# Three edits in the order of a hybrid decoder step: two heads' masked statistics change engine, one weight computation and one merge change step

## The chip, the cores and the metric

The kernel runs on one core of a Trainium2 chip. The metric is the device time of one execution in microseconds (us). The engines named below are TensorE (PE; its weight loads are shown as PEld), VectorE (DVE), ScalarE (ACT), GpSimd (POOL) and SyncE (SP), whose queue issues the DMA transfers of this kernel. Each engine works through its own list of instructions in the order in which the program wrote them.

## The reference

One layer of a decoder for a prompt of 2048 positions (width 1024) and for a sample group of 8 x 4 rows. The parts that the change is near:

```python
q, k, v, u, vg = _project(x, norm1_g, w_in)          # RMSNorm and one projection
for (w, d), bias_hj in zip(BRANCHES, biases):        # windows (128,1), (512,4), (2048,16)
    o, l = _dilated_prompt(q, k, v, bias_hj, d, w // d + 1)   # softmax(q k / 8 + bias) v, and its log-sum-exp
    outs.append(o); lses.append(l)
w = jax.nn.softmax(jnp.stack(lses, axis=0), axis=0)  # merge weights of each position and head
att = jnp.sum(w[..., None] * jnp.stack(outs, axis=0), axis=0)
x = x + jnp.concatenate([att, u * gate], axis=-1) @ w_out
x = x + _swiglu(x, norm2_g, w_gate, w_up, w_down)
```

There are 8 heads of 64 columns. After the layer comes a last RMSNorm. New key, value and gate caches are outputs too.

## The kernel before

**Stages.** Projection and gating come first (to some 430 us of the trace), then the attention of the sample group and of the prompt (to about 880 us), the output projection with the second RMSNorm (to about 960 us), and the feed-forward part, which goes through three blocks of positions (6, 6 and 4 tiles of 128) and takes the rest.

**How the attention is tiled.** The kernel folds the first two branches into one band of at most 5 tiles of 128 keys, and keeps the third, strided one apart; so each head has 16 band items (one for every 128 queries) and 4 strided items (4 residues of 16 each). A list holds all items of the 8 heads, 20 to a head, and item number i starts at step `B0 + i`. Heads are numbered 0 to 7; head 7 is the last one. Its list interleaves them: band 0, strided 0, band 1, strided 1, and so on to strided 3, then bands 4 to 15. Below, x is the step of head 7's first item, and L = x + 19 that of its last.

**What sets the order.** Every piece of work is registered with a step and a phase; the phases within a step are, in this order, early, exp, low, scores, turn, mid, values, out, misc, store. The plan sorts by step, phase and order of registration, and writes the instructions out in that order for all engines. So a piece registered earlier stands ahead on every engine that it uses, and an instruction that has to wait holds up what stands behind it on its engine.

**A band item.** Its scores (L856, PE into the two-buffer tile `ps_s`) come at its own step, the bias with the row minimum (L862, DVE) one step later, the exponential with the row sum (L867, ACT) two later, the transposition (L883, PE into a ring of three banks) three later with a copy of its first three blocks by ACT (L888), and of the others by DVE four later (L894). After each fourth band the products with the values follow (L911, PE, in two parts), and ACT copies them to the tile `ob` (L920). **A strided item** has POOL gather its keys and queries three steps ahead (L927, three casts into `sq`), scores (L935, PE), bias and minimum (L940, L942, DVE), a subtraction (L947, POOL), the exponential (L950, ACT), sums (L954, DVE), a transposition (L959, PE; L961, ACT), products (L971, PE) and a copy (L981, ACT).

**Statistics of a head** (class `Stats`). They bring the band's minima and sums into the strided item's layout and make the merge weights. Their pieces are: `a`, one product of the statistics with a selection mask into `sm` (L997, 128x256 for all 16 tiles of positions, 128x128 for 8 of them), on the engine named by its argument `eng`; `b`, four small matmuls (L1003, PE); `c`, four small DVE instructions (L1010 to L1013); `weights_e`, an exponential (L1016, ACT); `weights_b`, five small DVE instructions (L1021 to L1025); `store`, four DMA stores of the weights to the DRAM tensor `f_d` (L1031, SP). Heads 0 to 6 do this once. Head 7 does it in two halves: positions 0 to 1023 (`r0` is 0) at steps x+14 to x+16, positions 1024 to 2047 (`r0` is 64) at L+3 to L+6.

**The merge.** `merge_load` brings the weights back, spread over the partitions, a quarter of the positions (`ch`) at a time (L1045, SP). `merge` multiplies the band's and the strided output with them and adds (L1054, L1056, L1058), and `merge_store` writes the attention rows to the DRAM tensor `cat_d` (L1063, SP). Its last 128 rows are those of heads 6 and 7. For head 7, quarter 0 is merged by DVE and quarter 1 by POOL.

**The way into the output projection.** Tile 0 of `cat_d` is read by `load_cat` (L1340) without those last rows at step L-3, tiles 1 to 4 by `early_cat` (L1350): 7 of their 8 row groups long ahead, and the last one when head 7's first two quarters have been stored. `split_early` (L1357 ACT, L1358 DVE) and `split_cat` (L1364, L1365) make a high and a low part, in two halves of four row groups. PE multiplies them with `w_out` (L1373 to L1375): tile 0 in pieces from step L+2 on, then from step L+7 on `first_block` with tile 1, 2, 3, the rest of tile 0, 4 and 5. The parts of `w_out` are loaded (L1313) and split (L135 ACT, L138 POOL) from step L-12 on.

Of the kernel before, what the change touches and what calls it, by code (L numbers as in the profile page):

```python
# [23 lines left out]
KD = D // P  # L24
H = 8
# [17 lines left out]
class Plan:  # L43
# [8 lines left out]
    def at(self, step, phase, fn, *args):  # L52
        self.events.append((step, self.PHASES.index(phase), self.n, fn, args))
        self.n += 1
# [10 lines left out]
def hymba_step(ctx: ExitStack, tc: tile.TileContext, A: dict, O: dict):  # L65
    nc = tc.nc
    sync, act, dve, pool, pe = nc.sync, nc.scalar, nc.vector, nc.gpsimd, nc.tensor
# [7 lines left out]
    turn = [0, 0, 0, 0]  # L75
# [85 lines left out]
    at = plan.at  # L161
# [517 lines left out]
    for half in range(2):  # L679
        for ki, kind in enumerate(ORDER[half]):  # L680
            for gi, tiles in enumerate(GROUPS):
# [13 lines left out]
                for j, tj in enumerate(tiles):  # L695
                    t = half * 8 + tj
                    e, ph = e0 + 2 * j, "out"
                    if last:
                        e, ph = e0, "early"
                    elif third:  # L700

                        e, ph = (e0 + 2 * j + 2, "out") if j < 2 else (e0, "early")
# [45 lines left out]
    i = 0  # L748
# [44 lines left out]
    heads, loads, sts, fs, obs, o3s, spare = {}, {}, {}, {}, {}, {}, {}  # L793
# [333 lines left out]
    L = B0 + len(items) - 1  # L1127
# [13 lines left out]
            at(s0 + 5, "misc", finish_load, h)  # L1141
    def stats_of(h, steps, r0, r1):
        d = {}
        at(*steps[0], lambda: d.update(s=Stats(h, sts[h], r0, r1, dve if r0 else pool)))
        for (y, ph), fn in zip(steps, "a b c weights_e weights_b store".split()):
            at(y, ph, lambda fn=fn: getattr(d["s"], fn)())

    for h in range(H):

        s0 = B0 + (h + 1) * NI  # L1150
        end = h == H - 1
        ahead = h == H - 2
        if end:

            x = s0 - NI
            stats_of(h, [(x + y, ph) for y, ph in ((14, "early"), (14, "turn"), (15, "early"), (16, "early"), (16, "early"), (16, "mid"))], 0, 64)
            steps = ((2, "early"), (2, "turn"), (3, "early"), (4, "early"), (5, "early"), (5, "early"))
            at(x + 18, "mid", merge_load, h, 0)
            for part in range(3):
                at(x + 20 + part, "store", merge, h, 0, dve, part)  # L1160
                at(x + 21 + part, "store", merge, h, 1, pool, part)
            at(x + 24, "store", merge_store, h, 0, 2)
        else:
            steps = ((2, "misc"), (3, "misc"), (4, "early"), (5, "early"), (5, "misc"), (6, "mid"))

            for ch, (a, b) in enumerate(((8, 11), (8, 14), (11, 17), (11, 24) if ahead else (11, 20))):
                if ch % 2 == 0:
                    at(s0 + a, "mid", merge_load, h, ch)
                for part in range(3):
                    at(s0 + b + part, "store", merge, h, ch, pool, part)  # L1170
            if ahead:
                at(s0 + 17, "store", merge_store, h, 0, 2)
                at(s0 + 27, "store", merge_store, h, 2, 4)
            else:
                at(s0 + 23, "store", merge_store, h, 0, 4)
        stats_of(h, [(s0 + y, ph) for y, ph in steps], 64 if end else 0, P)
    for i, it in enumerate(items):
        x, h, n = B0 + i, it["h"], it["n"]
# [550 lines left out]
    B = blocks[0]  # L1729
# [40 lines left out]
    at(L + 1, "misc", split_cat, B, 0)  # L1770
    for i, y in ((1, -10), (2, -10), (3, -8), (4, -5)):
        at(L + y, "store", early_cat, B, i, 0, KD - 1)
        at(L + 5, "store", early_cat, B, i, KD - 1, KD)
    for j, ss in enumerate(((0, 1), (2,), (3,), (4, 5), (6,))):
        at(L + 2 + j, "misc", open_part, B, 0, ss, j == 0, False)

# [8 lines left out]
    h = H - 1  # L1785
# [150 lines left out]
    for bi, B in enumerate(blocks):  # L1936
# [8 lines left out]
        part = 4  # L1945
# [172 lines left out]
```

## Time and profile before

| what | value |
|---|---|
| device time, median of 3 runs | 2518.91 us (2518.27 to 2525.55) |
| device time of the profiled execution | 2524.36 us |
| its span, first to last instruction | 2522.5 us |
| PE busy | 2442.2 us, 97% of the span |
| DVE, ACT, POOL busy | 1269.3, 1129.8, 1291.3 us |
| mean granted TensorE clock | 0.988 |
| DMA, mean over the span | 181 GB/s |

A row of the timeline gives the start, the duration, the engine, the line of the kernel, the operation, what it writes and reads, and in square brackets the idle time of its engine just before, with what ended it. Consecutive instructions of one kind are put together (x4). The stretches give, for each engine, its busy time and its count of instructions, then the TensorE clock that was granted (1.00 is full), the DMA share and rate. Span and device time differ by what lies around the first and the last instruction, here 2524.36 - 2522.5 = 1.9 us.

### The profile page before, as it was taken

How to read it: one execution, taken by the hardware profiler on the slowest of the kernel's cores; microseconds unless marked ns; L12 is line 12 of the kernel's file. 1: busy time of each engine (PE TensorE's matmuls, PEld its weight loads, DVE VectorE, ACT ScalarE, POOL GpSimd, SP SyncE). 2: the span in 40 equal slices, each digit the busy share in tenths (PEclk: the TensorE clock that was granted, in tenths of full speed). 3: DMA queues.
4: the chain of work that ended last, by engine and by line, in shares of the span. 5: the costliest groups of instructions: out<-in, count | busy, mean ns of one | idle time of the engine just before them, and what ended most of it. 6: DMA issues, size and time to landing. Idle time of an engine off the chain costs nothing.

```text
span 2522.5 us, 39114 instructions
## 1 busy us (share of the span) xinstructions
PE 2442.2 (97%) x14022; PEld 2114.2 (84%) x14022; DVE 1269.3 (50%) x2601; ACT 1129.8 (45%) x2438; POOL 1291.3 (51%) x1010
## 2 busy tenths in 40 slices
PE   8998999999999888999999999999999999999996
PEld 6877776668888678899899888999999987999996
DVE  4558673216777634443444465444444466444445
ACT  6324343317666556445445455323323346344432
POOL 2216441004778546667667643543645534666662
PEclk9999999999999899999999999999999999999999
DMA  9874835676554463545545462653544644665552
GB/s 294 277 233 152 258 119 167 196 260 187 174 177 134 131 201 110 179 131 190 180 134 191 164 204 93 208 201 130 203 169 154 213 149 142 213 216 195 197 188 109
DMA packets 292148, 455.36 MB, mean 181 GB/s; under 512 B 28695, under 2 KB 160968, under 8 KB 286836
## 3 DMA queue, kind: packets, MB, share of 16 engines
q1 hardware_dynamic: 285108, 440.82, 53.4%
q10 hardware_dynamic: 6848, 12.06, 1.7%
q8 instruction: 111, 1.82, 0.3%
q14 instruction: 81, 0.66, 0.1%
HBM read 365.07 MB, written 157.84 MB: 207 GB/s over the span
## 4 chain that ended last, share of the span: by engine, by line
PE 57%; POOL 9%; issue 8%; DVE 3%; ACT 3%; DMA 2%; SPq 0%; POOLq 0%; DVEq 0%; ACTq 0%
PE ps_o L1679 13%; PE ps_m L1606 8%; PE ps_m L1607 8%; PE ps_m L1608 8%; POOL op L1549 3%; PE ps_s L856 2%; PE ps_o L911 2%; PE ps_t L883 1%; POOL dw L138 1%; PE ps_s L935 1%; PE ps_s L318 1%; DMA ab_d<-pair 1%; POOL pair L1529 1%; POOL fr L1532 1%; POOL pair L1538 1%
## 5 line engine op out<-in xcount | busy, mean ns | idle before, releaser
L1549 POOL TENSOR_TENSOR op<-fr,op 128x512 fp32r<-128x512 f32 x385 | 488.4, 1300 | 303.8 <-ACT op L1545 281.4
L1606 PE MATMUL ps_m<-xh,op 128*128 128x384 f32 (+3 forms) x1904 | 605.4, 318 | 5.2 <-DVE raw L1635 4.2
L1608 PE MATMUL ps_m<-xh,op 128*128 128x384 f32 (+3 forms) x1904 | 604.7, 318 | 0.0
L1607 PE MATMUL ps_m<-xl,op 128*128 128x384 f32 (+3 forms) x1904 | 604.1, 317 | 0.1
L1679 PE MATMUL ps_o<-dw,hw 128*128 128x512 f32 x2040 | 486.8, 392 | 8.8 <-DVE acc L1681 8.7
L1679 PEld LDWEIGHTS ps_o<-dw,hw 128*128 128x128 f32 x2040 | 378.7, 188 | 95.3 <-DVE acc L1681 14.6
L1606 PEld LDWEIGHTS ps_m<-xh,op 128*128 128x128 f32 x1904 | 360.1, 189 | 10.7 <-issue 5.6
L1607 PEld LDWEIGHTS ps_m<-xl,op 128*128 128x128 f32 x1904 | 360.0, 189 | 4.0 <-DVE xl L1462 0.4
L1608 PEld LDWEIGHTS ps_m<-xh,op 128*128 128x128 f32 x1904 | 359.8, 189 | 0.1
L1681 DVE TENSOR_TENSOR acc<-acc,ps_o 128x512 f32<-128x512 f32 (+1 forms) x362 | 247.3, 686 | 214.7 <-PE ps_o L1679 214.6
L1646 ACT ACTIVATE ps_t<-zn 128x384 f32<-128x384 f32 (+1 forms) x126 | 58.1, 461 | 435.3 <-DVE zn L1629 336.5
L1545 ACT ACTIVATE op<-fr 128x512 fp32r<-128x512 f32 x396 | 235.4, 623 | 24.3 <-DMA fr<-ab_d 14.9
L138 POOL TENSOR_TENSOR dw<-fd,dw 128x1024 fp32r<-128x1024 f32 x66 | 158.6, 2404 | 161.4 <-ACT dw L135 161.4
L318 PE MATMUL ps_s<-wh,xh 128*128 128x512 f32 x480 | 198.0, 412 | 6.4 <-ACT xh L135 6.4
L319 PE MATMUL ps_s<-wl,xh 128*128 128x512 f32 x480 | 189.8, 395 | 0.0
L320 PE MATMUL ps_s<-wh,xl 128*128 128x512 f32 x480 | 189.6, 395 | 0.0
L536 POOL TENSOR_TENSOR pr<-kv,qb 96x512 f32<-96x512 f32 x32 | 46.8, 1461 | 171.6 <-DMA kv<-in_cache_k_dram 101.8
L1656 ACT ACTIVATE hw<-ps_t 128x384 fp32r<-128x384 f32 (+1 forms) x126 | 56.2, 453 | 175.1 <-DVE ps_t L1652 174.1
L1517 ACT ACTIVATE fr<-fr,g2c 128x128 f32<-128x128 f32 x352 | 108.7, 388 | 56.8 <-DMA fr<-in_w_gate_dram 55.4
L318 PEld LDWEIGHTS ps_s<-wh,xh 128*128 128x128 f32 x480 | 91.5, 191 | 48.9 <-issue 23.7
L1549 POOL TENSOR_TENSOR op<-pair,op 128x512 fp32r<-128x512 f32 x63 | 81.1, 1296 | 96.9 <-ACT op L1545 96.9
L927 POOL CAST sq<-k 128x512 fp32r<-128x512 f32 x32 | 34.1, 1067 | 164.7 <-PE ps_s L319 164.7
(476 smaller groups left out, 4270.0 us busy)
## 6 DMA issues: line engine op xcount, KB each, us to landing
fr<-ab_d SPq DMA_DIRECT2D x308, 256.0 KB
fd<-in_w_down_dram SPq DMA_DIRECT2D x66, 512.0 KB
out_ks_dram<-in_cache_k_dram SPq DMA_DIRECT2D x56, 512.0 KB
out_vs_dram<-in_cache_v_dram SPq DMA_DIRECT2D x56, 512.0 KB
ab_d<-fr SPq DMA_DIRECT2D x88, 256.0 KB
qk_d<-pair SPq DMA_DIRECT2D x64, 256.0 KB
ab_d<-pair SPq DMA_DIRECT2D x63, 256.0 KB
kv<-in_cache_k_dram SPq DMA_DIRECT2D x64, 192.0 KB
```

What stands on the lines that cost most here:

```text
L138: (eng_lo or pool).tensor_sub(lo, src, hi.bitcast(F32))
L318: pe.matmul(o[j], xh[:, k, :], wh, start=(k == 0), stop=False)
L319: pe.matmul(o[j], xh[:, k, :], wl, start=False, stop=False)
L320: pe.matmul(o[j], xl[:, k, :], wh, start=False, stop=(k == KD - 1))
L1517: act.activation(w_[:, k * P:(k + 1) * P], w_[:, k * P:(k + 1) * P], AF.Copy, scale=g2c[:, kk:kk + 1])
L1545: act.activation(ops[f, j][0], ab[f][j], AF.Copy)
L1549: (pool if f or j in POOL_LOW else dve).tensor_sub(lo_, ab[f][j], hi.bitcast(F32))
L1606: pe.matmul(out, wh[:, ks], xh[:, :, k], start=(k == 0), stop=False)
L1607: pe.matmul(out, wh[:, ks], xl[:, :, k], start=False, stop=False)
L1608: pe.matmul(out, wl[:, ks], xh[:, :, k], start=False, stop=(k == 3))
L1679: pe.matmul(ps[0:nr], l_, r_[:, cs], start=(z == 0 and y == 0), stop=(z == FC - 1 and y == len(pairs) - 1))
L1681: dve.tensor_add(B.acc[i][0:nr, cs], B.acc[i][0:nr, cs], ps[0:nr])
```

## The change

Three things are edited.

- `a` of the statistics (L997) goes to DVE for head 6 and for the first half of head 7, where POOL did it. The second half of head 7 was on DVE already; heads 0 to 5 stay on POOL.
- For the first half of head 7, `weights_b` goes from step x+16 to x+17 (still phase early), its stores from x+16 to x+17 (phase mid). The exponential stays at x+16.
- DVE's merge of quarter 0 goes from steps x+20, x+21, x+22 (L+1 to L+3) to x+22, x+23, x+24 (L+3 to L+5), its store with that of quarter 1 from L+5 to L+6, and the four `early_cat` loads of the last row group likewise from L+5 to L+6.

```diff
     def stats_of(h, steps, r0, r1):
         d = {}
-        at(*steps[0], lambda: d.update(s=Stats(h, sts[h], r0, r1, dve if r0 else pool)))
+        at(*steps[0], lambda: d.update(s=Stats(h, sts[h], r0, r1, dve if h >= H - 2 else pool)))
...
-            stats_of(h, [(x + y, ph) for y, ph in ((14, "early"), (14, "turn"), (15, "early"), (16, "early"), (16, "early"), (16, "mid"))], 0, 64)
+            stats_of(h, [(x + y, ph) for y, ph in ((14, "early"), (14, "turn"), (15, "early"), (16, "early"), (17, "early"), (17, "mid"))], 0, 64)
             steps = ((2, "early"), (2, "turn"), (3, "early"), (4, "early"), (5, "early"), (5, "early"))
             at(x + 18, "mid", merge_load, h, 0)
             for part in range(3):
-                at(x + 20 + part, "store", merge, h, 0, dve, part)
+                at(x + 22 + part, "store", merge, h, 0, dve, part)
                 at(x + 21 + part, "store", merge, h, 1, pool, part)
-            at(x + 24, "store", merge_store, h, 0, 2)
+            at(x + 25, "store", merge_store, h, 0, 2)
...
         at(L + y, "store", early_cat, B, i, 0, KD - 1)
-        at(L + 5, "store", early_cat, B, i, KD - 1, KD)
+        at(L + 6, "store", early_cat, B, i, KD - 1, KD)
```

## The prediction

> **What bounds the kernel now.** The page first: the span, the engines, and the chain of work that ended last.
>
> ```profile
> span 2522.5 us, 39114 instructions
> PE 2442.2 (97%) x14022; PEld 2114.2 (84%) x14022; DVE 1269.3 (50%) x2601; ACT 1129.8 (45%) x2438; POOL 1291.3 (51%) x1010
> ...
> PE 57%; POOL 9%; issue 8%; DVE 3%; ACT 3%; DMA 2%; SPq 0%; POOLq 0%; DVEq 0%; ACTq 0%
> ```
>
> PE sets the time; a microsecond counts if PE gets through earlier. The edits lie in the last two heads, so next come the stretches around them: after the duration stand PE, PEld, DVE, ACT and POOL with their counts, the granted clock, the DMA share and GB/s.
>
> ```profile
> 821.00:831.00 10.00, 7.32 (x39) 5.26 (x36) 6.67 (x16) 2.15 (x7) 8.14 (x9) 0.66 0.23 54
> ...
> 847.00:851.00 4.00, 3.57 (x28) 3.10 (x29) 1.67 (x7) 0.81 (x2) 0.37 (x2) 0.60 1.10 278
> ...
> 857.50:861.00 3.50, 3.07 (x12) 3.07 (x13) 2.02 (x7) 1.92 (x5) 0.07 (x1) 0.57 0.17 31
> ...
> 870.00:875.00 5.00, 4.52 (x24) 2.82 (x24) 3.52 (x13) 0.61 (x2) 3.03 (x4) 0.67 0.26 53
> 875.00:880.00 5.00, 5.00 (x29) 3.56 (x28) 1.71 (x3) 2.65 (x6) 0.00 (x0) 0.99 0.28 73
> 880.00:918.00 38.00, 38.00 (x170) 31.41 (x168) 9.75 (x14) 12.83 (x31) 16.07 (x14) 1.00 0.73 223
> ```
>
> Four stretches of low clock stand out; from 875 to 918 PE is full, at full clock. The timeline of PE shows a stall ahead of each:
>
> ```profile
> 823.38 0.62 PE L1003 MATMUL ps_o<-sel_r,sm 128*128 128x16 f32 x4 [2.08 <-POOL sm L997]
> ...
> 847.43 0.41 PE L1003 MATMUL ps_o<-sel_r,sm 128*64 128x16 f32 x4 [2.16 <-POOL sm L997]
> ...
> 857.93 0.86 PE L856 MATMUL ps_s<-k,qh 128*128 128x384 f32 x2 [2.16 <-DVE st L862]
> ...
> 860.04 0.88 PE L856 MATMUL ps_s<-k,qh 128*128 128x384 f32 x2
> ...
> 870.48 0.59 PE L1003 MATMUL ps_t<-sel_r,sm 128*128 128x16 f32 x4 [1.85 <-DVE sm L997]
> ...
> 872.78 2.40 PE L911 MATMUL ps_o<-pt,v 128*64 128x256 f32 x12
> ...
> 876.00 1.30 PE L911 MATMUL ps_o<-pt,v 128*64 128x256 f32 x12
> ...
> 882.14 0.39 PE L1373 MATMUL ps_t<-op,accm 128*128 128x512 f32 x1
> ```
>
> The stalls sum to 2.08 + 2.16 + 2.16 + 1.85 = 8.25 us, and what follows runs slow: twelve L911 take 2.40 us at 872.78 and 1.30 at 876.00. The row at 882.14 is the first product of tile 1 that needs the second half of its split; I come back to it.
>
> **A, head 6's mask product to DVE.** One instruction leaves POOL and one joins DVE.
>
> ```profile
> 822.67 0.65 POOL L997 TENSOR_TENSOR sm<-st,sel_g 128x256 f32<-128x256 f32 x1
> ...
> 828.06 1.08 POOL L947 TENSOR_TENSOR e<-e,st 128x512 f32<-128x512 f32 x1
> ```
>
> ```profile
> 824.10 0.18 DVE L1010 TENSOR_TENSOR ps_o<-ps_o,st 128x16 f32<-128x16 f32 x1 [4.48 <-PE ps_o L1003]
> ...
> 826.98 2.20 DVE L1021 TENSOR_TENSOR dd<-f,s 128x16 f32<-128x16 f32 x1
> ...
> 869.31 1.02 DVE L997 TENSOR_TENSOR sm<-st,sel_g 128x256 f32<-128x256 f32 x1
> ```
>
> POOL reached L997 only at 822.67, behind three casts. DVE then sat 4.48 us before L1010, so from 819.6 on it has room for an instruction of 0.65 (POOL's row) to 1.02 us (DVE's row for the second half). The mask is then ready before PE's idle begins at 823.38 - 2.08 = 821.3: PE gains 2.1 us there and some of the slow clock. What is late next is POOL: its subtraction L947 at 828.06 moves by only the 0.65 us that L997 frees, and `weights_b` on DVE starts with a 2.20 us instruction, where the same kind takes 0.17 without company; it ends at 829.18, just after POOL's L947 (828.06 + 1.08 = 829.14). The next strided bias stands behind it. So A lies between 0.65 us (POOL's saving alone) and 3.1 us (stall, plus about 1 us of slow L911); as POOL feeds this stretch I take **1.5**. The Trainium skill, "SBUF — State Buffer", section "Who interferes with whom", says that a DVE instruction with two SBUF inputs and a GpSimd instruction that reads SBUF take turns, each blocked for the other's whole length; the ends at 829.14 and 829.18 agree. By that rule the moved L997 may hold POOL as long as it did before, and A would be nearer 0.65.
>
> **B, the same for head 7's first half, and C, its `weights_b` a step later.** The rows on POOL, ACT and DVE:
>
> ```profile
> 846.97 0.40 POOL L997 TENSOR_TENSOR sm<-st,sel_g 128x128 f32<-128x128 f32 x1
> ```
>
> ```profile
> 843.78 0.83 ACT L867 ACTIVATE e<-e,st 128x640 f32<-128x640 f32 x1
> ...
> 850.68 0.63 ACT L135 ACTIVATE op<-v 128x512 fp32r<-128x512 f32 x1 [1.49 <-DMA v<-in_w_out_dram]
> ```
>
> ```profile
> 853.44 1.24 DVE L1021 TENSOR_TENSOR dd<-f,s 64x16 f32<-64x16 f32 x1 [3.15 <-ACT f L1016]
> ...
> 855.88 0.93 DVE L1025 TENSOR_TENSOR f<-f 64x32 f32<-64x32 f32 x1
> ...
> 857.06 0.80 DVE L862 CUSTOM_DVE_ANT_0 e<-ps_s,b 128x640 f32<-128x640 f32 x1
> ```
>
> On DVE, L997 has to wait for the exponential of band 7 (843.78 + 0.83, some 844.7 with its sum); a band copy and a bias are queued behind it for about 0.9 us. PE gets its mask at about 845.8, 1.6 us earlier than 847.43. But ACT then stands at its split of `w_out`, whose transfer lands at 850.68 in a stretch where DMA is full (share 1.10), and later exponentials stand behind that. So B alone lies between 0 and 1.6 us. C removes the chain that follows: DVE waited 3.15 us for the exponential of the weights, its five instructions ended at 856.81, the bias at 857.06 came after them, and PE stood 2.16 us for it. One step later the bias goes first. PE was ready for its next scores at 857.93 - 2.16 = 855.8, and with 1.4 us of B's head start left it begins them at 854.4. `weights_b` now holds the bias after that: from 853.4 (the exponential is no earlier) for the same 3.4 us to 856.8, bias (0.80) to about 857.7 with a copy ahead of it, so the following scores start at 857.7 instead of 860.04: 2.3 us, of which I carry 2.1 on. B and C together: **2.1**, from 0 (ACT's wait paces all) to 3.9 (`weights_b` in 1 us, without POOL beside it).
>
> C also moves SP. The stores of the weights now stand behind `load_cat` of tile 0; so it goes out by 856.8 instead of 859.15; the stores and the reload behind them stay about where they were:
>
> ```profile
> 856.83 2.28 SPq L1031 DMA_DIRECT2D f_d<-f  x4
> 859.15 0.46 SPq L1340 DMA_DIRECT2D pair<-cat_d  x1
> ...
> 861.85 0.63 SPq L1045 DMA_DIRECT2D zn<-f_d  x1
> ...
> 871.47 1.27 SPq L1063 DMA_DIRECT2D cat_d<-ob  x2
> 874.00 0.33 SPq L1350 DMA_DIRECT2D ob<-cat_d  x1
> ...
> 875.96 2.27 SPq L1031 DMA_DIRECT2D f_d<-f  x4
> 878.35 0.86 SPq L1340 DMA_DIRECT2D xl<-cat_d  x2
> ```
>
> **D, the merge two steps later.** Three DVE instructions move behind the second half's L997 (two of them) and behind its L1010 to L1013:
>
> ```profile
> 870.59 0.79 DVE L1058 TENSOR_TENSOR ob<-ob,o 128x256 f32<-128x256 f32 x1
> ...
> 872.12 0.17 DVE L1021 TENSOR_TENSOR dd<-f,s 128x16 f32<-128x16 f32 x1
> ...
> 873.46 0.19 DVE L1025 TENSOR_TENSOR f<-f 128x32 f32<-128x32 f32 x1
> ```
>
> L997 no longer queues behind L1054 and L1056 (869.31) but follows the last exponential, which in my walk ends at 865.5; its 1.02 us fit beside PE's first products, and the 1.85 us stall goes. So does the slow clock after it: 2.40 - 1.30 = 1.1 us of L911, and some 0.7 in the small matmuls before. D is **3.7**, from 1.85 (stall alone) to 3.7.
>
> **E, what the order of SP gives back.** Before, the merge ended at 870.59 + 0.79 = 871.38 and the store went out at 871.47. After, DVE ends the merge near 870.6 by B to D, 869.1 with A. But the store now stands at L+6, phase store, and the second half's `f_d` stores at L+6, phase early: they are ahead in SP's queue, and wait for `weights_b` of that half, which stands behind the merge. That adds 1.5 us (872.12 to 873.65) and the 2.27 us of four issues. The store goes at 872.9, and the last row group, 874.00 - 871.47 = 2.5 us behind it, at 875.4. A load of that size lands within 2.4 us (878.35, used by ACT at 880.76 without a wait):
>
> ```profile
> 880.76 0.29 ACT L1364 ACTIVATE xh<-xl 128x128 fp32r<-128x128 f32 x1
> ```
>
> The far bound is the 4.85 us from 861.85 to POOL's use of that load:
>
> ```profile
> 866.70 1.28 POOL L1054 TENSOR_TENSOR ob<-ob,zn 128x256 f32<-128x256 f32 x1 [1.84 <-DMA zn<-f_d]
> ```
>
> With 2.4 us and 0.6 us of split, PE can pass the product of 882.14 at 878.4. By A to D (1.5 + 2.1 + 3.7 = 7.3 us) it would be there at 874.8. So the gain is cut to 882.14 - 878.4 = 3.7 us, and a new stall of 3.6 us stands where none was. All earlier stalls of about 2 us were followed by a low clock; after 870.48 that cost 1.8 us. Net gain: 3.7 - 1.8 = **1.9 us**. The Trainium skill, "TensorE: Matmul & The Clock Gate", section "What's actually happening", states that the clock halves after an idle window of about 3.4 us; here stalls of 1.85 to 2.16 us were enough (0.57 to 0.67), so the measurement decides. By the page's figure the new stall would be at the border, and without a drop the sum would be 3.7.
>
> After 882 PE is dense to 918, and the rest follows PE; `w_out`'s other half is split early enough for a start a few us sooner, so I carry 1.9 us to the end: 2524.36 - 1.9 = 2522.5 for the profiled execution. That execution lay 5.45 us above the median of the runs; the same gain there gives 2518.91 - 1.9 = **2517.0 us**. No row bears on losses elsewhere, as no other instruction is edited.
>
> **The rivals.** R1, the `cat_d` chain is not late (DVE finishes early, or loads land sooner): PE keeps 7.3 us, or 8.9 with A at its far end: 2511.6 to 2510.0. For it speaks that the edits reach all four stalls; against it, the order of SP's queue. R2, the old feeders decide: POOL's casts give A only 0.65, ACT's `w_out` wait swallows B and C, and E takes D: 2518.3. For it speaks the full POOL up to 829 and DMA share 1.10. R3, slower: the mechanism is E alone, from the point where the last row group lands after 881.5. With 4.85 us of landing and 2.2 us more of blocked DVE instructions (L1021's row) it lands at 875.4 + 4.85 + 2.2 = 882.5, PE passes at 883.1, 1.0 us later than before, and 1.8 us of low clock follow: 2521.7. Against it: its loads are a quarter of the size.
>
> **How the numbers follow.** The forecast has 0.50, R1 0.17, R2 0.20, R3 0.13. About 0.3% (7.6 us) is what a measurement of this kernel can tell from no change: below 2511.4 or above 2526.5. Only R1's upper part lies beyond it on the fast side, 0.13; on the slow side R3 would have to lose thrice its price, 0.05; the rest, 0.82, is within. The range is R1's far end to R3 with the spread that the three runs show above their median at a small weight: 2510 to 2523.
>
> **What would show it.** A: no PE idle at the first L1003, DVE's L1010 without 4.48 us. B, C: L1003 near 1.6 us earlier, ACT's `w_out` wait longer, no idle at the scores after. D: L1003 of the second half without a stall. E: four `f_d` stores ahead of the `cat_d` stores, and a PE stall of some 3.6 us in the middle of tile 1, ended by ACT's L1357. It is wrong if that stall is absent and PE keeps over 7 us, or if the row group lands after 881.5.

## The result, and the profile after

The changed kernel takes 2526.03 us (median of 20 runs, 2521.3 to 2534.36), the kernel before 2520.16 us (20 runs, 2514.6 to 2525.55) in the same comparison. The ratio is 1.0022, with an interval of 1.0014 to 1.0030: slower by about 5.5 us, where the forecast was a gain of 1.9 us, and above the range that was given. Of the distance between 2526.03 and the forecast of 2517.0 us, 1.25 us lie in the base: the kernel before has a median of 2520.16 us over 20 runs, where the prediction had 2518.91 from three. The profiled execution of the changed kernel took 2529.22 us. Its page, the same three lines as for the kernel before (span; engines; chain of waits by engine):

```profile
span 2527.4 us, 39118 instructions
...
PE 2438.7 (96%) x14022; PEld 2111.6 (84%) x14022; DVE 1275.7 (50%) x2603; ACT 1128.9 (45%) x2438; POOL 1288.6 (51%) x1008
...
PE 56%; POOL 9%; issue 8%; DVE 4%; ACT 3%; DMA 1%; SPq 0%; POOLq 0%; ACTq 0%; DVEq 0%
```

PE is busy for 3.5 us less than before (2438.7 against 2442.2) and the span is 4.9 us longer. So PE waits more. The stretches of the changed kernel, columns as in the prediction:

```profile
821.00:831.00 10.00, 2.81 (x18) 1.99 (x12) 9.33 (x10) 1.46 (x4) 6.83 (x8) 0.78 0.23 52
847.00:851.00 4.00, 3.75 (x38) 3.08 (x37) 2.12 (x7) 4.00 (x11) 3.81 (x5) 1.00 0.93 230
857.50:861.00 3.50, 3.29 (x28) 2.42 (x26) 3.40 (x6) 3.06 (x9) 3.50 (x4) 1.00 0.48 122
883.00:888.00 5.00, 4.99 (x14) 3.67 (x15) 4.49 (x8) 3.28 (x7) 0.00 (x0) 0.66 0.76 200
883.00:921.00 38.00, 37.99 (x159) 30.83 (x159) 10.79 (x15) 13.90 (x33) 15.97 (x14) 0.96 0.73 227
```

Two of the old stretches of low clock are gone (847 and 857.5 now have 1.00). The same work comes some 4 us later here, and in the stretches that match, 851 to 855 and 861.5 to 865, the clock is 1.00 too. Two losses are new. From 821 to 831 PE is busy for only 2.81 us of 10 while DVE is busy for 9.33. After 883, where the clock had been full, it is 0.66. The timeline of PE in the changed kernel shows what stands ahead of each (start, duration, and in brackets the idle time before and what ended it):

```profile
828.26 1.00 PE L1003 MATMUL ps_o<-sel_r,sm 128*128 128x16 f32 x4 [6.59 <-DVE sm L997]
...
851.04 0.38 PE L1003 MATMUL ps_o<-sel_r,sm 128*64 128x16 f32 x4 [0.29 <-DVE sm L997]
...
855.58 1.30 PE L911 MATMUL ps_o<-pt,v 128*64 128x256 f32 x12 [1.51 <-ACT o L981]
...
861.88 0.56 PE L856 MATMUL ps_s<-k,qh 128*128 128x384 f32 x2 [1.09 <-DVE st L862]
...
869.71 0.51 PE L1003 MATMUL ps_t<-sel_r,sm 128*128 128x16 f32 x4
...
883.01 0.50 PE L1373 MATMUL ps_t<-op,accm 128*128 128x512 f32 x1 [3.15 <-ACT accm L1357]
```

Of the four old stalls (2.08, 2.16, 2.16, 1.85) the first has grown to 6.59, the second has shrunk to 0.29, the third to 1.09 with 1.51 for another reason ahead of it, and the fourth is gone. The stall of 3.15 us in the middle of tile 1 is new. It ends where ACT gets the last row group of `cat_d`. The timelines of SP and of ACT in the changed kernel show that chain:

```profile
852.03 3.12 SPq L1340 DMA_DIRECT2D pair<-cat_d  x1
...
875.45 2.27 SPq L1031 DMA_DIRECT2D f_d<-f  x4
877.83 1.26 SPq L1063 DMA_DIRECT2D cat_d<-ob  x2
880.40 0.33 SPq L1350 DMA_DIRECT2D ob<-cat_d  x1
```

```profile
867.91 0.82 ACT L867 ACTIVATE e<-e,st 128x640 f32<-128x640 f32 x1
...
882.33 0.63 ACT L1357 ACTIVATE accm<-ob 128x512 fp32r<-128x512 f32 x1 [6.50 <-DMA ob<-cat_d]
```

The four `f_d` stores now stand ahead of the `cat_d` store. The store goes out at 877.83 (871.47 before), the reload at 880.40 (874.00 before), and ACT waits 6.50 us for it. DVE, in the changed kernel:

```profile
819.24 8.87 DVE L997 TENSOR_TENSOR sm<-st,sel_g 128x256 f32<-128x256 f32 x1
...
871.90 1.02 DVE L1058 TENSOR_TENSOR ob<-ob,o 128x256 f32<-128x256 f32 x1
872.85 0.71 DVE L1021 TENSOR_TENSOR dd<-f,s 128x16 f32<-128x16 f32 x1
...
874.77 0.65 DVE L1025 TENSOR_TENSOR f<-f 128x32 f32<-128x32 f32 x1
...
921.28 0.69 DVE L1384 TENSOR_TENSOR acc<-acc,ps_o 128x512 f32<-128x512 f32 x1 [9.80 <-PE ps_o L1375]
```

Head 6's mask product, which was costed at 0.65 to 1.02 us, took 8.87. The merge ends at 871.90 + 1.02 = 872.92, and `weights_b` stands between it and the stores until 874.77 + 0.65 = 875.42.

So there were two suspects from the first look: the 8.87 us of A, and the place of the store, E. The larger number turned out not to be the cause.

### The profile page after: what moved, and what is told of

Read it like the earlier page. It is cut to its first block, busy times and chain, and to the rows that moved or that the text cites. A ratio compares the mean times of both kernels' runs of the same rounds, so it can differ in the third digit from the quotient of the medians.

```text
span 2527.4 us, 39118 instructions
## 1 busy us (share of the span) xinstructions
PE 2438.7 (96%) x14022; PEld 2111.6 (84%) x14022; DVE 1275.7 (50%) x2603; ACT 1128.9 (45%) x2438; POOL 1288.6 (51%) x1008
## 4 chain that ended last, share of the span: by engine, by line
PE 56%; POOL 9%; issue 8%; DVE 4%; ACT 3%; DMA 1%; SPq 0%; POOLq 0%; ACTq 0%; DVEq 0%
PE ps_o L1679 13%; PE ps_m L1608 8%; PE ps_m L1607 8%; PE ps_m L1606 8%; POOL op L1549 4%; PE ps_s L856 3%; PE ps_o L911 2%; PE ps_t L883 1%; POOL dw L138 1%; PE ps_s L935 1%; POOL pair L1529 1%; POOL fr L1532 1%; POOL pair L1538 1%; PE ps_s L318 1%; PE ps_o L1373 1%
## 5 line engine op out<-in xcount | busy, mean ns | idle before, releaser
L1606 PE MATMUL ps_m<-xh,op 128*128 128x384 f32 (+3 forms) x1904 | 605.9, 318 | 7.2 <-DVE raw L1635 5.4
L1606 PEld LDWEIGHTS ps_m<-xh,op 128*128 128x128 f32 x1904 | 360.7, 189 | 13.0 <-issue 7.0
```

The costliest lines, as they stand in the source:

```text
L1606: pe.matmul(out, wh[:, ks], xh[:, :, k], start=(k == 0), stop=False)
```

## The experiments

Each comparison has its own runs of the kernel before on the same chip; their median stands behind the slash. "After" is the changed kernel. The letters A to E are those of the prediction.

### Head 6's product back on POOL (after without A), and the store back ahead as well (without A and E)

The first kernel is the changed one with this edit:

```
-dve if h >= H - 2 else pool
+dve if h == H - 1 else pool
```

> The change without its part A: head 6's mask product stays on POOL, all else as changed. Theory P (the loss is A: the DVE product with two SBUF operands starves beside POOL's unbroken row of instructions, 8.87 us instead of about 1): the 6.59 us PE idle before the first L1003 becomes the 2.08 us of before, and the time is 1 to 4 us below the kernel before, with a PE stall of 2 to 4 us still in the middle of tile 1. Rival Q (the loss is the order of SP's queue, E): the time stays 4 to 6 us above the kernel before.

The second has that edit and these two:

```
-            at(x + 25, "store", merge_store, h, 0, 2)
+            at(x + 24, "store", merge_store, h, 0, 2)
...
-        at(L + 6, "store", early_cat, B, i, KD - 1, KD)
+        at(L + 5, "store", early_cat, B, i, KD - 1, KD)
```

> As the run without A, and head 7's merge store and the last row group's loads go back to step L+5, ahead of the second half's weight stores in SP's queue; the merge on DVE keeps its late steps. If E works as the prediction says, the store goes out 3.5 to 4 us sooner after the merge, the stall in the middle of tile 1 shrinks from 2 to 4 us to under 1 us, and the time falls by 2 to 5 us below the run without A. If the stall has another cause (the loads' own landing, the split on ACT), the time equals the run without A within 1 us.

Without A: 2527.09 / 2522.16 us, ratio 1.0019 (1.0010 to 1.0028). The loss is still there although the stall of 6.59 us is not. PE of this kernel:

```profile
824.56 0.62 PE L1003 MATMUL ps_o<-sel_r,sm 128*128 128x16 f32 x4 [2.07 <-POOL sm L997]
...
854.18 2.40 PE L911 MATMUL ps_o<-pt,v 128*64 128x256 f32 x12 [4.15 <-ACT o L981]
...
883.12 0.50 PE L1373 MATMUL ps_t<-op,accm 128*128 128x512 f32 x1 [2.84 <-ACT accm L1357]
```

Without A and E: 2518.98 / 2522.16 us, ratio 0.9992 (0.9983 to 1.0001). The two kernels differ only in the step of the store and of the reload, and the medians by 8.1 us, more than the 2 to 5 us expected; the intervals do not touch. SP and ACT of the second kernel:

```profile
872.75 1.27 SPq L1063 DMA_DIRECT2D cat_d<-ob  x2
...
875.28 0.33 SPq L1350 DMA_DIRECT2D ob<-cat_d  x1
...
877.23 2.27 SPq L1031 DMA_DIRECT2D f_d<-f  x4
```

```profile
877.21 0.63 ACT L1357 ACTIVATE accm<-ob 128x512 fp32r<-128x512 f32 x1 [2.23 <-DMA ob<-cat_d]
```

The store is ahead of `f_d` again, ACT waits 2.23 us instead of 6.20, and PE has no idle in tile 1. That the loss is A's falls here, and that it is the order in SP's queue holds. The first kernel shows something else: with B and C in place PE waits 4.15 us for ACT's copy of a strided output, L981. ACT stands in front of that at its split of `w_out`:

```profile
853.23 0.63 ACT L135 ACTIVATE op<-v 128x512 fp32r<-128x512 f32 x1 [4.83 <-DMA v<-in_w_out_dram]
```

Before, this wait was 1.49 us. The same shows in all four kernels that have B and C without the long product of head 6 (this pair, and below the whole change with the mask in PSUM, with and without E): the L1003 of head 7's first half came 1.6 to 3.7 us earlier after head 6's last exponential than in the three profiles of the kernel before (27.96 to 29.60 us against 31.17 to 31.70), and yet this L135 began at 34.4 to 35.8 us, where it had been 34.1 to 34.9. ACT waited 4.5 to 5.0 us for it and PE 3.8 to 4.4 us for ACT. The time that B saves is waited for here.

### Head 6's product alone on DVE (A alone)

The kernel before, with this edit; one kernel timed, and the same program profiled once more.

```
-dve if r0 else pool
+dve if r0 or h == H - 2 else pool
```

> The kernel before with part A alone: only head 6's mask product goes to DVE. Theory P: that instruction takes 8 to 9 us again and ends when POOL's row of instructions ends; PE idles some 6.5 us before the first L1003; the time is 4 to 6 us above the kernel before. Rival Q: within 1 us of the kernel before, or below it by the 1.5 us that the prediction gave to A.

> The kernel before with part A alone once more, the same program as the run with head 6 only, for one more profile. Theory S: the duration of head 6's product on DVE is a matter of chance, between 1 us (as in that profile) and 9 us (as in the changed kernel's), and the first L1003 waits accordingly. Rival: 1.0 to 1.2 us again, so that the 8.87 us belongs to the changed kernel alone.

A alone: 2522.15 / 2522.16 us, ratio 1.0004 (0.9992 to 1.0016). In the profile of this kernel, DVE's timeline:

```profile
817.72 1.17 DVE L997 TENSOR_TENSOR sm<-st,sel_g 128x256 f32<-128x256 f32 x1
```

In the second execution (2524.01 us), by the view of groups of that window (minimum, median, maximum in ns):

```profile
L997 DVE TENSOR_TENSOR sm<-st,sel_g x1: 8875/8875/8875, 818.2 to 818.2; 128x256 f32<-128x256 f32 x1
```

One program, 1.17 us in one execution and 8.88 in another. So the length is decided from execution to execution. The end of the attention (the last L920) came at 55.55 us after head 6's last exponential with 1.17 us and at 61.29 with 8.88, and the two executions took 2519.23 and 2524.01 us. One pair does not make this the product's price: executions of the kernel before lie as far apart (below). In the changed kernel POOL's timeline beside it is one unbroken row:

```profile
819.25 0.90 POOL L1056 TENSOR_TENSOR o<-o,pair 128x256 f32<-128x256 f32 x1
...
826.79 1.04 POOL L927 CAST sq<-ql 128x512 fp32r<-128x512 f32 x1
831.41 1.04 POOL L947 TENSOR_TENSOR e<-e,st 128x512 f32<-128x512 f32 x1 [3.58 <-DVE st L942]
```

Nine POOL instructions run from 819.25 to 827.83 (826.79 + 1.04), and DVE's L997, begun at 819.24, ends at 828.11, just after the last. In the execution with 1.17 us it got in after the first of them.

### Head 6's mask in PSUM

To see whether it is DVE's second SBUF operand that POOL holds up, ACT copies head 6's mask (8 columns, 0.18 us) to PSUM, and L997 reads it there. Once in the changed kernel, once with A alone in the kernel before:

```
+    def mask_psum():
+        p = ps_a(); act.activation(p[:, 64:72], sel_g, AF.Copy)
+        return p, p[:, 64:72]
...
-            n = self.r1 // 8
+            n = self.r1 // 8; self.p, sel = mask_psum() if self.h == H - 2 else (None, sel_g)
...
-                              sel_g.unsqueeze(1).unsqueeze(1).broadcast_to([P, 2, n, 8]), op=OP.mult)
+                              sel.unsqueeze(1).unsqueeze(1).broadcast_to([P, 2, n, 8]), op=OP.mult)
...
-            self.p = pt = ps_a()
+            self.p = pt = ps_a() if self.p is None else self.p
```

> The whole change, but head 6's product on DVE reads the mask from PSUM, where ACT has copied its 8 columns just before (one short ACT instruction more), so that it has one operand in SBUF. It is otherwise the same instruction at the same place. Theory P: it takes 0.4 to 1 us beside the same POOL row, the 6.59 us PE idle goes, and the time is at or below that of the run without A, 2 to 6 us below the kernel before. Rival R (the instruction is slow for another reason than its second SBUF operand: its statistics come late, or DVE itself): still 8 to 9 us and the time of the changed kernel.

> The kernel before with part A alone, in the form that reads the mask from PSUM (one ACT copy of 8 columns more): nothing else of the change. Theory S (A's product on DVE is worth something, but beside POOL's row it starves in some executions, which is why A alone moved nothing in the median): with one SBUF operand it takes 0.4 us in every execution, and the time is 2 to 6 us below the kernel before. Rival T (what A gains is taken up by the transfers of w_out that ACT waits for, so it is worth nothing however fast it is): within 1.5 us of the kernel before.

In the changed kernel with the mask in PSUM, by the view of groups:

```profile
L997 DVE TENSOR_TENSOR sm<-st,ps_t x1: 422/422/422, 814.1 to 814.1; 128x256 f32<-128x256 f32 x1
```

0.42 us here, in the other kernel of the pair and in the one of the last experiment, with POOL as busy as before. So the second SBUF operand was the reason for the long product. The times: whole change with the mask in PSUM 2525.29 / 2522.16 us, 1.0013 (1.0004 to 1.0021); A alone in this form 2522.04 / 2523.25 us, 0.9990 (0.9980 to 1.0001). The first, expected 2 to 6 us below the kernel before, is still slower than it, although PE no longer idles at head 6's L1003, and its PE timeline has the stall of tile 1 unchanged:

```profile
875.80 0.54 PE L1373 MATMUL ps_t<-op,accm 128*128 128x512 f32 x1 [3.20 <-ACT accm L1357]
```

### E alone, and D alone

The kernel before with only the store and the reload a step later (`x + 25`, `L + 6`), so that only SP's order differs:

```
-            at(x + 24, "store", merge_store, h, 0, 2)
+            at(x + 25, "store", merge_store, h, 0, 2)
...
-        at(L + 5, "store", early_cat, B, i, KD - 1, KD)
+        at(L + 6, "store", early_cat, B, i, KD - 1, KD)
```

> The kernel before with E's part alone: head 7's merge store and the last row group's loads go from step L+5 to L+6, which puts the second half's four weight stores ahead of them in SP's queue; the merge and all else stay. The programs differ in the order of SP's queue only. Theory Q (this order is the loss): the store goes out some 4.5 us later (the end of the weights at 873.65, four issues of 0.57 us), the row group lands near 882, PE stalls in tile 1, and the time is 2 to 6 us above the kernel before. Rival (the row group had that much slack): within 1 us.

The kernel before with only the merge on DVE two steps later, so that only DVE's order differs:

```
-                at(x + 20 + part, "store", merge, h, 0, dve, part)
+                at(x + 22 + part, "store", merge, h, 0, dve, part)
```

> The kernel before with D alone: DVE's merge of quarter 0 two steps later, the store and the last row group's loads where they were (L+5, ahead of the weight stores), so that only DVE's order differs. Theory U (the stall at the second half's L1003 is near 0.9 us as a rule, and the store now waits for a later merge): 0 to 2 us below the kernel before, with the row group landing 1 to 3 us later and no stall in tile 1. Rival (D as the prediction has it, 3.7 us): 3 to 5 us below.

E alone: 2525.03 / 2523.25 us, 1.0005 (0.9995 to 1.0016). D alone: 2520.23 / 2524.66 us, 0.9988 (0.9976 to 1.0000). PE with E alone, then with D alone:

```profile
864.57 0.59 PE L1003 MATMUL ps_t<-sel_r,sm 128*128 128x16 f32 x4 [0.93 <-DVE sm L997]
...
876.52 0.50 PE L1373 MATMUL ps_t<-op,accm 128*128 128x512 f32 x1 [1.71 <-ACT accm L1357]
```

```profile
868.01 0.51 PE L1003 MATMUL ps_t<-sel_r,sm 128*128 128x16 f32 x4
...
878.01 0.39 PE L1373 MATMUL ps_t<-op,accm 128*128 128x512 f32 x1
```

By the ratios E alone is 1.3 us above the kernel before (1.3 below to 4.0 above), less than the 2 to 6 us expected, and D alone 3.0 us below (0 to 6), which fits 0 to 2 us as well as the 3 to 5 of the prediction. In the profiles, E by itself makes the stall in tile 1 (1.71 us), D by itself takes the stall of the second half's L1003 away and makes none. Neither alone costs what both cost. D and E together without B and C were not run, nor B and C without D.

### The two kernels profiled again

The kernel before twice, the changed one once more, without an edit, to see how much of a stall is the execution's own.

> The kernel before, unchanged, for a second profile. The run with the store late alone differs from it only in SP's queue behind step L+5, yet its PE was 4.6 us further at the end of the attention than in the profile that the prediction read (56.5 against 61.1 us after the exponential of head 6's last band). Theory U (the profiled execution was late in this stage, and part of the 8.25 us of stalls is not there as a rule): PE's stalls ahead of the scores at step x+17 and of the second half's L1003 are near 0.8 and 0.9 us instead of 2.16 and 1.85, and the end of the attention lies at 56 to 58 us. Rival (the stalls are the rule): 60 to 62 us again.

> The kernel before once more, for a third profile, with the same two theories: 56 to 58 us if the profiled execution was late, 60 to 62 us if not; one of each if chance sets it from execution to execution.

> The changed kernel once more, for a second profile. The duration of head 6's product on DVE may come out anywhere from 1 to 9 us; theory Q holds that the end is the same either way, because the last row group lands 64 to 66 us after the exponential of head 6's last band, after which PE ends its stall in tile 1 (65 to 67 us). If head 6's product sets the time, a short one brings PE there 4 us sooner.

The kernel before took 2519.70 and 2522.22 us in these, the changed one 2529.56. The stalls of the changed kernel came again (6.61 and 3.24 us; L997 8.89 us). Those of the kernel before did not all: in the first of its two new profiles PE shows

```profile
854.79 0.56 PE L856 MATMUL ps_s<-k,qh 128*128 128x384 f32 x2 [0.98 <-DVE st L862]
...
865.23 0.59 PE L1003 MATMUL ps_t<-sel_r,sm 128*128 128x16 f32 x4 [0.92 <-DVE sm L997]
```

where the profile behind the prediction had 2.16 and 1.85. The other one had 2.12 and 1.85. The last L920 came at 56.35 and 60.04 us after head 6's last exponential, one in each of the two ranges expected.

### The whole change, mask in PSUM, store back ahead

The edits of the mask in PSUM above, on the changed kernel, with `x + 24` and `L + 5` for the store and the reload: everything but E.

> The whole change with both repairs: head 6's mask read from PSUM, and head 7's merge store with the last row group's loads at L+5, ahead of the second half's weight stores. Theory S: the gains add up, 5 to 9 us below the kernel before. Rival T: no more than the run with the store ahead gave by itself, 2 to 4 us below the kernel before. In both the stall in the middle of tile 1 is under 1.5 us.

2520.08 / 2523.25 us, ratio 0.9984 (0.9971 to 0.9997). It differs from the whole change with the mask in PSUM (1.0013) only by E. That is 4.0 us below the kernel before, the 2 to 4 us of the second theory and not the 5 to 9 of the first. It is the only kernel here whose interval lies wholly below 1; D alone (0.9988) is not to be told apart from it.

## Why the prediction was wrong

**The step that failed.** The sum credited A to D with 1.5 + 2.1 + 3.7 = 7.3 us by the time PE reaches the product of tile 1, and let E take 5.4 us of them. E did what was predicted and cost about as much or more. The gains in front of it did not come: without E the runs gave 4.0 us (0.9984, mask in PSUM; 0.8 to 7.3) and 2.0 us (0.9992, without A; -0.3 to 4.3) instead of 7.3. By the traces the failed terms are A, B and C, whose 3.6 us never reached the last exponential, because ACT's wait for `w_out` took them (and the long product of A was added), and in D the size, 1.0 us in most executions instead of 3.7.

**A clock for the end of the attention.** The start of the stage differs by a few us between executions of one program, so the profiles are set against a mark of their own: the start of the last band's exponential (L867 on ACT, 867.91 in the row of the changed kernel above, 866.67 before). A second mark is the start of head 6's last exponential, ahead of which nothing is edited. ACT, before and then changed:

```profile
816.26 0.82 ACT L867 ACTIVATE e<-e,st 128x640 f32<-128x640 f32 x1
...
866.67 0.82 ACT L867 ACTIVATE e<-e,st 128x640 f32<-128x640 f32 x1
```

```profile
816.62 0.82 ACT L867 ACTIVATE e<-e,st 128x640 f32<-128x640 f32 x1
```

The table counts from the first mark. In us after it, it gives: when ACT begins the split that the product of tile 1 needs (the second L1357); when PE could have begun that product (its start less its idle time); when it did; and when DVE began its third addition of the output projection, L1384, which ends the work that all this holds up. In the changed kernel that is 882.33 - 867.91 = 14.42, 883.01 - 3.15 - 867.91 = 11.95, 15.10, and 921.28 - 867.91 = 53.37.

| kernel | split | PE ready | product | L1384 |
|---|---|---|---|---|
| before, the profile of the prediction | 11.48 | 15.47 | 15.47 | 51.71 |
| before, again | 9.21 | 12.95 | 12.95 | 49.19 |
| before, a third time | 9.90 | 13.88 | 13.88 | 50.12 |
| A alone, twice, and in the PSUM form | 9.14 to 9.16 | 12.94 to 12.97 | 12.94 to 12.97 | 49.18 to 49.21 |
| D alone | 10.01 | 11.80 | 11.80 | 48.04 |
| B, C, D (without A and E) | 10.45 | 12.11 | 12.11 | 48.87 |
| whole change, PSUM, without E | 9.89 | 11.81 | 11.81 | 48.05 |
| E alone | 14.15 | 13.12 | 14.83 | 51.50 |
| B to E (without A) | 14.13 | 11.97 | 14.81 | 53.03 |
| whole change, PSUM | 14.49 | 11.97 | 15.17 | 53.23 |
| whole change | 14.42 | 11.95 | 15.10 | 53.37 |
| whole change, again | 14.50 | 11.95 | 15.18 | 53.41 |

Wherever E is in, the split comes at 14.1 to 14.5, elsewhere at 9.1 to 11.5. Wherever D is in, PE is ready at 11.8 to 12.1. From the product to L1384 it takes 36.24 us in all profiles without a stall but one (36.76), 36.67 after the stall of 1.71, and 38.1 to 38.3 after stalls of 2.84 and more.

**E: the right mechanism, 4.2 us later than forecast.** The prediction had this order in SP's queue, the stall, its place and its end. It gave the stall 3.6 us and the low clock after it 1.8; measured were 3.15 and 2.0 (38.27 - 36.24). What failed is the time at which PE passes the product: 878.4 by the sum, 883.01 in the trace. Line up the two traces by the mark at head 6 (816.26 before, 816.62 after), and 883.01 is 882.65: 4.2 us late. By its terms: the merge on DVE ends at 872.92 (872.56 so lined up) instead of 869.1, 3.5 us late. `weights_b` of the second half and the four issues take 877.83 - 872.92 = 4.9 instead of 1.5 + 2.27 = 3.8 us, 1.1 late; the five instructions take 2.5 us, the first 0.71 where the row of before had 0.17. Store to reload takes 2.57 (2.5 in the prediction). From there to ACT's use it is 1.93 instead of 2.4, which gives 0.5 back. So 3.5 of the 4.2 us lie ahead of the merge, where A, B and C should have gained. The price of E itself was about right: against the same kernel without it, E costs 53.03 - 48.87 = 4.2 us and 53.23 - 48.05 = 5.2 us by the table, and by the runs, times 2520, 6.8 us (1.0019 against 0.9992) and 7.3 us (1.0013 against 0.9984), to within 3 to 4 us. The prediction's sum had 7.3 - 1.9 = 5.4.

**A, B and C: 3.6 us that did not come.** These are the 3.5 us by which the merge ended late, since the merge follows the last band's exponential. It began 51.29 us after the mark at head 6 (867.91 - 816.62), no earlier than before (50.41, 48.18 and 50.94 in its three profiles). In all six profiles with B and C this distance is 49.2 to 51.3 us, in the eight without 47.4 to 53.1. B did what was predicted at its place: with A undone L1003 came at 29.56 us after that mark, 31.17 to 31.70 before, and DVE waited 0.93 to 0.99 us for the exponential. C took the stall at the scores away where A was undone, and left 1.09 us in the changed kernel, where before had 2.16, 0.98 and 2.12. But ACT's wait for `w_out` grew from 1.49 to 4.83 us without A (2.20 in the changed kernel, whose long product had used up the head start), and PE lost the time again in a stall of 4.15 us (1.51). This is the second rival, the old feeders, which had 0.20. Taken together B and C are worth nothing that the runs can see: 0.9988 with D alone, 0.9992 with B, C and D. Intervals of about 2.5 us to either side would hide the 2.1 us, so that they came to nothing rests on the traces.

**A's 8.87 us, and why they cost little.** The step "from 819.6 on it has room for an instruction of 0.65 to 1.02 us" took idle time on DVE for room. The prediction drew on the Trainium skill, "SBUF — State Buffer", section "Who interferes with whom", on DVE with two SBUF inputs against GpSimd, and drew from it only that POOL might be held up. The trace agrees with the rule, and it was DVE that was held up, over nine instructions of POOL and not one (8.87 us); with one operand in PSUM it took 0.42 us. PE's L1003 came at 11.64 us after the mark at head 6, 4.5 us later than before (7.12). At the L1003 of head 7's second half the changed kernel was at 53.09 us, and the four with B to D but without the long product at 51.01 to 52.65: 0.4 to 2.1 us are left of the 4.5, because those four had waited 3.8 to 4.4 us for ACT in between, against 1.51. Alone, A gave 1.0004 in its plain form and 0.9990 in PSUM, both with intervals that hold 1; the whole change gave 1.0022, without A 1.0019 and with the mask in PSUM 1.0013. So the long product may be up to some 2 us of the loss (2.3 by 1.0022 against 1.0013, whose intervals overlap), but most of the loss stands without it. Whether the short form gains the 1.5 us forecast, the runs cannot tell.

**D: 3.7 us for one execution, less for most.** D took the stall at the second half's L1003 away, as predicted. The term was a stall of 1.85 us and 1.8 us of low clock after it, both read off one profile. Against the profile that the prediction used, PE was ready 15.47 - 11.95 = 3.5 us earlier, close to the term. But that profile was the latest of seven with the old place of the merge. In the other six PE was ready at 12.94 to 13.88, so D is worth 1.0 to 1.9 us there (1.0 in four of them). Five of the seven had a stall of 0.92 or 0.93 us. The third profile of the kernel before had 1.85 us again, but the clock behind it was 1.00 (868.6 to 873.6) and not 0.67, and PE was ready at 13.88. With D alone a stall of 2.41 us at the scores (858.67) was followed by 1.00 as well. That stalls of about 2 us are followed by a low clock, as the prediction has it, held in its own profile and not in every one. Runs gave D alone 3.0 us, with an interval from 0 to 6. It also takes away what had covered E: with E alone PE waits 1.71 us for the last row group, with D beside it 3.15, and only the longer stall is followed by 2 us of low clock.

**The sum again.** With what the runs gave: A about 0, B and C about 0, D a gain of 1 to 3, E a cost of 4.2 to 7.3. That makes a loss of 1.2 to 6.3 us, and the measured one is 5.5 (3.5 to 7.6). By the table it is 53.4 - 49.2 = 4.2 us against the usual execution of the kernel before. What is left, 1.3 us, lies within the interval. The feed-forward part, which is not edited, took 1568.1 and 1567.6 us in the two profiles of the changed kernel, from its first product (L1606) to the end of the span, and 1566.0 to 1567.4 in the three of the kernel before; over all profiles it lies between 1565.8 and 1569.3 without an order that the edits explain, and this stays open.

**The rivals.** The result is the third one's, slower, by its mechanism E, which had 0.13, with the last row group used at 882.33, past its point of 881.5. The price of 2521.7 came from a slow landing (4.85 us) and a blocked DVE. The landing was quick (1.93 us). The lateness came from the gains of A to C that were missing ahead of it. The chance of 0.05 for slower by over 0.3% took R3's price as its middle and so bore on a loss of 7.6 us; a loss of 5.5 us is within that bound and still outside the range, which ended at 2523 because the second and the third rival were not added up: each was costed as if the other's terms held.

## What to carry to other kernels

When a store with its reload moves to a later step, write down which transfers then stand ahead of it in the same queue, what those wait for, and how long the reload may be late; an earlier consumer uses that slack up, so the two edits must be costed together. A gain that has to pass another engine's wait (here ACT's for `w_out`) is none until that wait moves too, and a rival that says so is to be run through the other rivals' sums. One profile's stall of 2 us may be 1 us in most executions (here 1.85 in two of seven, 0.92 in five), and the low clock behind it may be missing: profile the kernel before more than once before adding stalls up.

## What the runs showed of the hardware

A DVE product with two SBUF operands beside an unbroken row of POOL instructions took 8.87, 8.89 and 8.88 us in three profiles and 1.17 in a fourth, where POOL's cast beside it took 1.29 us instead of 1.05; with one operand in PSUM 0.42 us in three. In the three it ended only with the last of nine POOL instructions, so one instruction of the other engine is no bound for the wait.

The stall of 3.15 us in tile 1 was followed by a granted clock of 0.66 for 5 us, and cost 2.0 us on top of itself. The three others at that place, of 2.84 to 3.24 us, were followed by 0.66 too. The stall of 1.71 us with E alone was followed by 1.00 and cost 0.4 (36.67 against 36.24). Between these lengths it went both ways: 1.85 us ahead of the second half's L1003 was followed by 0.67 in one execution of the kernel before and by 1.00 in another.

The same program ran the end of the attention in times that differ by 4.7 us (last output copy L920 at 61.09, 56.35 and 60.04 us after the mark in head 6, three profiles of the kernel before). That is about as much as the whole change was worth. The stalls at the scores and at the second half's L1003 and the low clock behind them are part of it; what chooses between them was not found.
